# A recurrence's triangular inverse in 16x16 blocks, and its state updated in one pass

## The chip, the cores and the metric

The kernel runs on one core of one Trainium2 chip. The core has a matrix engine (TensorE, PE in the profile), a vector engine (VectorE, DVE), an activation engine (ScalarE, ACT), a general engine (GpSimd, POOL) and SyncE (SP), which here only issues DMAs. Each engine works through its own instructions in order, and semaphores tie the engines together. The metric is the device time of one execution in microseconds, the median of several runs.

## The reference

A two-layer diffusion backbone runs over 512 latent and 256 context tokens of width 1024, batch 1. Each layer normalizes, projects its input to three token mixers and three gates, merges the mixers by the gates, and ends with a SwiGLU block. The third mixer is the one changed, a bidirectional recurrence with 8 heads of 64:

```python
def step(S, inp):                                   # one token
    w_t, k_t, v_t, kk_t, a_t = inp[:5]
    sa = jnp.einsum('bhvk,bhk->bhv', S, kk_t)
    S = S * w_t[:, :, None, :] - sa[..., None] * (kk_t * a_t)[:, :, None, :] + v_t[..., None] * k_t[:, :, None, :]
    return S, jnp.einsum('bhvk,bhk->bhv', S, inp[5])
```

It runs forward and backward, first over the context, then from that state over the latents.

## The kernel before

The kernel doesn't step by tokens. Tokens are taken in chunks of 32, four chunks to a group of 128, so that each direction (`f`, `b`) has six groups and 24 chunks (`SEQ`). Within a chunk the subtraction of `sa` couples the 32 tokens; it becomes a product with the inverse of a triangular 32x32 matrix for each head.

Class `Rwkv` does this with generators that run beside each other:

- `loads` and `prep` fetch a group's decays and keys, scale them, and make `X`: the products of keys within a chunk (`xp` on PE, masked by DVE), 128 rows, with the triangular matrices in its columns 0 to 31. `tp` and `bkt` are the keys transposed. The products go to the PSUM slot `a`, two banks, shared by `xp`, `tp` and the tails.
- `invert` takes a pair of groups, one of each direction, which hold 32 matrices a direction (4 chunks, 8 heads). It sends the matrices through DRAM (`d1`) into `L`, where each stands on 4 partitions; in `G` each of the 4 holds every fourth row of the inverse. `G` starts as the unit matrix, loaded anew. Then come 31 steps on DVE: multiply a column of `G` by a row of `L` into `ftmp`, subtract from `G`. `G` goes through DRAM (`d2`) into `TT`, in the layout that PE wants. Each step needs the one before.
- `chain` is the recurrence, chunk by chunk. PE makes `yp` from the values and from the state `S` (`sblkf`, `sblkb`), ScalarE negates it into `ysb`, PE multiplies by the inverse (`up`), ScalarE copies that to `uv`, PE makes the increment `sp`, and DVE adds it to the state's decayed copy `sc` (L1751). The copy is made as soon as the old state stands, by DVE, GpSimd or ScalarE (L1716, L1719). `op` and `ys` are the outputs.
- `tails` normalize and gate the outputs (`ty`, `gp`).

Beside them, `Kern.beside` runs the big products that fill PE: 16 gate projections (`px` over the 512 latents and, in layer 0 alone, `pz` over the context), then 8 branch projections over the first two mixers' outputs, whose operands `y` are loaded when the gates are done. Each product is three matmuls, of a high and a low part of both factors. A half weight unit is loaded to `raw`, split by ScalarE (`wh`) and by DVE or GpSimd (`wl`); it serves 12 `px`.

Class `Flow` sets the order. Each generator yields an `Op` with its engine, an assumed cost, what it reads and writes, and which slots it takes and gives. Flow takes the operation that could begin first by its own accounting, with a bias for each generator (`F.add(gen, bias, first)`; `first` counts until the first state is written). Engines then follow that order. What follows Flow in a layer is the third branch's projection (`last_branch`), which needs the tails.

Of the kernel before, what the change touches and what calls it, by code (L numbers as in the profile page):

```python
# [28 lines left out]
class Kern:  # L29
# [457 lines left out]
    def beside(self, F, l, n, W):  # L487

        nc, I = self.nc, self.I
        for tag, bufs in (("raw", 3), ("w", 2), ("gx", 2), ("gat", 3)):  # L490
            F.slot(tag, bufs)
# [4 lines left out]
        def raw():  # L496
            for j, src in enumerate(srcs):
                for e in range(2):
                    yield Op("SP", 0.55, (), ("raw", j, e), take=(("raw", (j, e)),), lat=3.5)
                    raws[j, e] = W.tile([128, 512], F32, name="raw", tag="raw", bufs=3)  # L500
                    nc.sync.dma_start(raws[j, e], src[:, 512 * e:512 * e + 512])
# [781 lines left out]
class Rwkv:  # L1283
# [40 lines left out]
    def open(self):  # L1324
        K, nc, l, I = self.K, self.nc, self.l, self.I
        e = self.ctx.enter_context
        self.P = P = e(K.pool(f"rP{l}", side="right"))
        self.T2 = e(K.pool(f"rE{l}", side="right"))
        self.T = self.ctx_t.enter_context(K.pool(f"rT{l}", side="right"))
        self.ps = e(K.pool(f"rps{l}", space=PSUM))  # L1330
        def ld(name, shape, src):
            t = P.tile(shape, F32, name=name)
            nc.sync.dma_start(t, src)
            return t
        self.wg2 = ld("wg2", [128, 512], I["wg2"][l])
        self.gnw = ld("gnw", [128, 128], I["gnw"][l])
        self.gnb = ld("gnb", [128, 128], I["gnb"][l])
        self.masks = ld("rmask", [128, 2, 64], I["rmask"])
        self.smask = P.tile([128, 16, 34], F32, name="smask")
# [174 lines left out]
    def streams(self, F):  # L1514

        self.n = n = {"f": 2 if self.zout else 3, "b": 3}
        for d in "fb":
            for tag, bufs in (("cp", 1), ("kr", n[d]), ("bk", 1), ("pc", 4), ("X", n[d]), ("bkt", 2), ("TT", 2), ("uv", 2), ("ysb", 1), ("ys", 2)):
                F.slot(tag + d, bufs)
        for tag, bufs in (("cs", 1), ("a", 2), ("yu", 2), ("o", 1), ("s", 1), ("d1", 4), ("d2", 4), ("L", 1), ("G", 1), ("tail", 2)):  # L1520
            F.slot(tag, bufs)
# [4 lines left out]
        for d in "fb":  # L1526
            F.add(self.loads(d), 0.15, 1.5)
        for d in "fb":
            F.add(self.chain(d), 0.0)
        for d in "fb":  # L1530
            F.add(self.load_v(d), 0.0)
            F.add(self.prep(d), 0.2, 1.5)
        F.add(self.invert(), 0.2, 1.5)
        F.add(self.tails(), 0.4)
# [29 lines left out]
    def prep(self, d):  # L1564
# [6 lines left out]
        for i, g in enumerate(self.SEQ[d]):  # L1571
# [15 lines left out]
            last = 32 if d == "f" else 1  # L1587
            E = yield Op((("DVE", 0.9), ("POOL", 1.5)), 0, (k("Pe"), k("kr")), k("krn"), take=(("pc" + d, i),))
            kr = h["kr"]
# [28 lines left out]
            for e in range(2):  # L1618
                yield Op("DVE", 0.7, (k("xp%d" % e),), k("X%d" % e), give=(("a", k(e)),), psum=True)
                if not e:  # L1620
                    X = h["X"] = T.tile([128, 2, 2, 4, 64], F32, name="X", tag="X" + d, bufs=self.n[d])
                nc.vector.tensor_tensor(out=X[:, e, :, :, 0:nI].rearrange("q w p i -> q (w p) i"), in0=xp[e][:, :, 0:nI],
# [15 lines left out]
    def invert(self):  # L1638


        nc, T = self.nc, self.T
        for i in range(6):
            k = lambda name, d="": (name, d, i)
            gs = {d: self.SEQ[d][i] for d in "fb"}
            yield Op("ACT", 0.45, (), k("G"), take=(("G", i),), lat=3.3)
            G = T.tile([128, 2, 8, 32], F32, name="G", tag="G", bufs=1)
            nc.scalar.dma_start(G, self.I["gid"])
            d1, L = {}, None
            for z, d in enumerate("fb"):
                g = gs[d]  # L1650
                for q in range(2):
                    yield Op("SP", 0.55, (("X1", d, g),), k("d1%d" % q, d), take=() if q else (("d1", k(0, d)),), lat=3.7)
                    if not q:
                        d1[d] = self.D.tile([2, 16, 32, 32], F32, name="d1", tag="d1", bufs=4)
                    X = self.hs[d, g]["X"]
                    r0 = 0 if q == 0 else 96
                    nc.sync.dma_start(d1[d][q].rearrange("u j i -> j u i"), X[r0:r0 + 32].rearrange("j e w p i -> j (e w p) i")[:, :, 0:32])
                yield Op("SP", 0.55, (k("d10", d), k("d11", d)), k("L", d), take=() if z else (("L", i),), give=(("d1", k(0, d)),), lat=4.2)
                L = L or T.tile([128, 2, 32, 32], F32, name="L", tag="L", bufs=1)
                nc.sync.dma_start(L[:, z].rearrange("u j i -> u (j i)"), d1[d].rearrange("q u j i -> (q u) (j i)").unsqueeze(1).to_broadcast([32, 4, 1024]))  # L1660
            tmp = None
            for n in range(31):
                a, m = n // 4 + 1, 31 - n
                yield Op("DVE", 2 * (0.158 + 0.00105 * 2 * a * m), (k("L", "f"), k("L", "b"), k("G")), k("T"), give=(("L", i),) if n == 30 else ())
                if tmp is None:
                    tmp = T.tile([128, 256], F32, name="ftmp", tag="ftmp", bufs=1)
                t = tmp[:, 0:2 * a * m].rearrange("q (d a b) -> q d a b", d=2, b=m)
                o = G[:, :, 0:a, n + 1:32]
                nc.vector.tensor_tensor(out=t, in0=G[:, :, 0:a, n:n + 1].to_broadcast([128, 2, a, m]), in1=L[:, :, n:n + 1, n + 1:32].to_broadcast([128, 2, a, m]), op=ALU.mult)  # L1669
                nc.vector.tensor_tensor(out=o, in0=o, in1=t, op=ALU.subtract)  # L1670
            for z, d in enumerate("fb"):
                for s in range(4):
                    yield Op("SP", 0.55, (k("T"),), k("d2%d" % s, d), take=() if s else (("d2", k(0, d)),), give=(("G", i),) if s == 3 and z else (), lat=2.5)
                    if not s:
                        d2 = self.D.tile([8, 4, 32, 32], F32, name="d2", tag="d2", bufs=4)
                    nc.sync.dma_start(d2.rearrange("m p (a s) i -> s (m p) a i", s=4)[s], G[s::4, z])
                yield Op("SP", 0.55, tuple(k("d2%d" % s, d) for s in range(4)), ("TT", d, gs[d]), take=(("TT" + d, i),), give=(("d2", k(0, d)),), lat=3.4)
                TT = self.hs[d, gs[d]]["TT"] = T.tile([128, 8, 32], F32, name="TT", tag="TT" + d, bufs=2)
                nc.sync.dma_start(TT, d2.rearrange("m p r i -> (p r) m i"))

    def chain(self, d):
# [3 lines left out]
        for i, g in enumerate(self.SEQ[d]):  # L1685
# [3 lines left out]
            for n in range(4):  # L1689
# [21 lines left out]
                nc.scalar.mul(ysb, yp, -1.0)  # L1711
                if S is not None:
                    E = yield Op((("DVE", 0.75), ("POOL", 1.36), ("ACT", 1.56)), 0, (("S", d),), k("sc"))
                    if E == "ACT":
                        for p in range(4):
                            nc.scalar.activation(self.sc[d][:, p, :], S[:, p, :], AF.Copy, scale=pc[:, p, cl:cl + 1])  # L1716
                    for e in range(0 if E == "ACT" else 2):
                        rr = slice(64 * e, 64 * e + 64)
                        (nc.vector if E == "DVE" else nc.gpsimd).tensor_tensor(out=self.sc[d][rr, :, 64 * e:64 * e + 64], in0=S[rr, :, 64 * e:64 * e + 64],  # L1719
                                                in1=pc[rr, :, cl:cl + 1].to_broadcast([64, 4, 64]), op=ALU.mult)  # L1720
                yield Op("PE", 0.2, (k("ysb"), ("TT", d, g)), k("up"), take=(("yu", k(1)),), give=(("ysb" + d, k(0)),))
# [30 lines left out]
                self.st[d] = Sn  # L1752
# [217 lines left out]
def _consts():  # L1970
# [23 lines left out]
    C["rmask"] = m  # L1994
    g = np.zeros((128, 2, 8, 32), f)
    for s_ in range(4):
        for a in range(8):
            g[s_::4, :, a, 4 * a + s_] = 1
    C["gid"] = g

    T = np.arange(512)
# [117 lines left out]
```

## Time and profile before

| | |
|---|---|
| median of 3 runs | 3251.05 us (3240.05 to 3264.98) |
| profiled execution, its own time | 3247.46 us |
| span of its trace | 3245.6 us |
| mean granted TensorE clock | 0.934 |
| PE busy | 2951.2 us (91%) |
| DVE busy | 1760.7 us (54%) |
| ACT busy | 1202.0 us (37%) |
| POOL busy | 558.7 us (17%) |

A busy share is an average over stages that have different limits. The two stretches in which Flow's order runs lie at about 658 to 1097 us (layer 0) and 2353 to 2756 us (layer 1). The span is from the first to the last instruction, 1.9 us less than the execution's time. [...]

### The profile page before, as it was taken

The numbers are of one execution on the slowest core, as the hardware profiler recorded it, in microseconds if no ns is written. First come the engines' busy times: TensorE is split into PE (matmuls) and PEld (weight loads), VectorE is DVE, ScalarE is ACT, GpSimd is POOL, SyncE is SP. The second block draws the span as 40 slices with busy tenths as digits, with TensorE's granted clock in tenths as the row PEclk, the third lists the DMA queues.
The fourth block names the chain that finished last, engine by engine and source line by source line (L and its number), as shares of the span: only waits on it lengthen the run. The fifth ranks groups of instructions, "written<-read, shape, count | busy, mean of one in ns | idle before, by whom it ended". The sixth has DMA issues, their size and how long they took to land. (4 is left out here: it accounts for less than half of the span.)

```text
span 3245.6 us, 62087 instructions
## 1 busy us (share of the span) xinstructions
PE 2951.2 (91%) x25760; PEld 2362.6 (73%) x25760; DVE 1760.7 (54%) x3455; ACT 1202.0 (37%) x2498; POOL 558.7 (17%) x429
## 2 busy tenths in 40 slices
PE   6999999879989889999999899889779887899998
PEld 3777877657767678888888787667556665888887
DVE  3185666766786745222223536646567767653335
ACT  3154454435443333212112434444335444332223
POOL 3033212200001222101001203212200111220102
PEclk9999999889989989999999899989889885899999
DMA  7421322355455542443222322213365652623333
GB/s 292 159 77 59 105 73 106 106 168 157 144 161 163 163 159 91 147 160 134 62 65 79 106 78 82 76 69 104 134 187 162 183 154 62 201 72 98 93 102 117
DMA packets 276282, 398.30 MB, mean 123 GB/s; under 512 B 96928, under 2 KB 178592, under 8 KB 276000
## 3 DMA queue, kind: packets, MB, share of 16 engines
q1 hardware_dynamic: 250528, 360.77, 34.9%
q10 hardware_dynamic: 25472, 33.56, 3.1%
q8 instruction: 202, 3.31, 0.4%
q14 instruction: 80, 0.66, 0.1%
HBM read 320.33 MB, written 73.92 MB: 121 GB/s over the span
## 5 line engine op out<-in xcount | busy, mean ns | idle before, releaser
L50 PE MATMUL px<-hh,wh 128*128 128x512 f32 x1584 | 644.3, 407 | 14.8 <-ACT gat L473 4.6
L50 PE MATMUL px<-hl,wh 128*128 128x512 f32 x1584 | 636.8, 402 | 9.2 <-POOL hl L302 7.9
L50 PE MATMUL px<-hh,wl 128*128 128x512 f32 x1584 | 636.8, 402 | 5.8 <-DVE wl L510 3.1
L71 ACT ACTIVATE wh<-raw 128x1024 fp32r<-128x1024 f32 (+1 forms) x266 | 275.5, 1039 | 722.4 <-PE pz L50 375.6
L72 DVE TENSOR_TENSOR wl<-raw,wh 128x1024 fp32r<-128x1024 f32 (+1 forms) x266 | 333.0, 1253 | 341.5 <-ACT wh L71 311.5
L50 PEld LDWEIGHTS px<-hh,wh 128*128 128x128 f32 x1584 | 304.3, 192 | 105.3 <-issue 25.8
L50 PEld LDWEIGHTS px<-hh,wl 128*128 128x128 f32 x1584 | 304.1, 192 | 81.6 <-issue 8.0
L50 PEld LDWEIGHTS px<-hl,wh 128*128 128x128 f32 x1584 | 304.1, 192 | 77.3 <-POOL hl L302 13.1
L50 PE MATMUL pz<-hh,wl 128*128 128x256 f32 x872 | 250.7, 288 | 1.3 <-DVE wl L72 0.8
L50 PE MATMUL pz<-hh,wh 128*128 128x256 f32 x872 | 249.9, 288 | 2.1 <-DVE fs L729 1.4
L50 PE MATMUL pz<-hl,wh 128*128 128x256 f32 x872 | 250.0, 287 | 1.9 <-DVE hl L304 1.4
L739 POOL TENSOR_TENSOR al<-fs,ah 128x768 fp32r<-128x768 f32 (+1 forms) x44 | 85.0, 1931 | 727.8 <-ACT ah L738 727.8
L50 PE MATMUL px<-y,wh 128*128 128x512 f32 (+1 forms) x512 | 158.8, 395 | 35.1 <-ACT y L123 13.6
L50 PEld LDWEIGHTS pz<-hh,wh 128*128 128x128 f32 x872 | 167.3, 192 | 10.9 <-issue 2.3
L50 PEld LDWEIGHTS pz<-hl,wh 128*128 128x128 f32 x872 | 168.1, 193 | 9.1 <-issue 2.0
L50 PEld LDWEIGHTS pz<-hh,wl 128*128 128x128 f32 x872 | 168.0, 193 | 6.0 <-issue 3.9
L50 PEld LDWEIGHTS px<-y,wh 128*128 128x128 f32 x512 | 96.1, 211 | 58.7 <-ACT y L123 14.3
L1736 ACT COPY uv<-up 32x128 f32<-32x128 f32 x384 | 98.1, 255 | 69.6 <-PE up L1727 57.6
L50 PE MATMUL px<-ah,wh 128*128 128x512 f32 x296 | 116.1, 393 | 0.0
L1670 DVE TENSOR_TENSOR G<-G,ftmp 128x120 f32<-128x120 f32 (+24 forms) x372 | 108.8, 293 | 12.8
L1669 DVE TENSOR_TENSOR ftmp<-G,L 128x120 f32<-128x120 f32 (+24 forms) x372 | 107.3, 288 | 15.4 <-DMA L<-d 5.3
L50 PE MATMUL px<-ah,wl 128*128 128x512 f32 x296 | 115.3, 390 | 0.0
(460 smaller groups left out, 5776.1 us busy)
## 6 DMA issues: line engine op xcount, KB each, us to landing
raw<-w SPq DMA_DIRECT2D x104, 512.0 KB, 3.5
araw<-wada SPq DMA_DIRECT2D x96, 512.0 KB, 5.0
raw<-win SPq DMA_DIRECT2D x82, 512.0 KB, 3.5
raw<-w SPq DMA_DIRECT2D x48, 448.0 KB, 3.4
raw<-win SPq DMA_DIRECT2D x64, 256.0 KB, 3.4
kr<-krd SPq DMA_DIRECT2D x24, 512.0 KB, 4.9
L<-d SPq DMA_DIRECT2D x24, 512.0 KB, 4.5
gs<-gat ACTq DMA_DIRECT2D x24, 384.0 KB, 3.1
```

Of the source, the lines that this page charges most:

```text
L50: return self.nc.tensor.matmul(out, lhsT=lhsT, rhs=rhs, start=start, stop=stop)
L71: nc.scalar.activation(h[:, :n], raw[:, :n], AF.Copy)
L72: nc.vector.tensor_tensor(out=lo[:, :n], in0=raw[:, :n], in1=h[:, :n].bitcast(F32), op=ALU.subtract)
L739: nc.gpsimd.tensor_tensor(out=al, in0=s, in1=ah.bitcast(F32), op=ALU.subtract)
L1669: nc.vector.tensor_tensor(out=t, in0=G[:, :, 0:a, n:n + 1].to_broadcast([128, 2, a, m]), in1=L[:, :, n:n + 1, n + 1:32].to_broadcast([128, ...
L1670: nc.vector.tensor_tensor(out=o, in0=o, in1=t, op=ALU.subtract)
L1736: nc.scalar.copy(uv[ru, p].rearrange("q e v -> q (e v)"), up[32 * p:32 * p + 32, :])
```

## The change

There are four parts.

1. `invert` works on the two 16x16 blocks on the diagonal of each 32x32 matrix. The 64 blocks of a direction have 2 partitions each, `L` shrinks to a quarter and `G` to a half, and 15 steps replace 31. The blocks go to fixed DRAM tensors that are zeroed at the start of the layer, so that `TT` arrives with both inverses on its diagonal and zeros beside them. Twice as many smaller DMAs write `d1`.
2. A new generator, `finish`, makes the remaining block for each group and direction, as inverse times block times inverse: `ep` transposes `TT` by PE, `qp` multiplies by `X`, `fp` by `TT` once more, with copies by ScalarE between (`E`, `Q`), and a DVE pass adds the result to `TT` with the sign in `other`.
3. In `chain` the decayed copy is gone. DVE updates each of the state's four columns of heads by one pass that multiplies by the decay and adds the increment, on 64 partitions at a time: eight passes for two additions.
4. Numbers: `raw` has two buffers instead of three, `kr` and `X` of the forward direction in layer 0 three instead of two, the lead `first` is 1.0 instead of 1.5, and one GpSimd cost is 1.0 instead of 1.5.

```diff
-        for tag, bufs in (("raw", 3), ("w", 2), ("gx", 2), ("gat", 3)):
+        for tag, bufs in (("raw", 2), ("w", 2), ("gx", 2), ("gat", 3)):
...
-        self.n = n = {"f": 2 if self.zout else 3, "b": 3}
+        self.n = n = {"f": 3, "b": 3}
...
-        F.add(self.invert(), 0.2, 1.5)
+        F.add(self.invert(), 0.2, 1.0)
+        for d in "fb":
+            F.add(self.finish(d), 0.1, 1.0)
...
-            for n in range(31):
-                a, m = n // 4 + 1, 31 - n
-                yield Op("DVE", 2 * (0.158 + 0.00105 * 2 * a * m), (k("L", "f"), k("L", "b"), k("G")), k("T"), give=(("L", i),) if n == 30 else ())
+            for n in range(15):
+                a, m = n // 2 + 1, 15 - n
+                yield Op("DVE", 2 * (0.17 + 0.0012 * 2 * a * m), (k("L", "f"), k("L", "b"), k("G")), k("T"), give=(("L", i),) if n == 14 else ())
...
+    def finish(self, d):
...
+        for i, g in enumerate(self.SEQ[d]):
+            k = lambda name: (name, d, i)
+            yield Op("PE", 0.9, (k("D"),), k("ep"), take=(("a", k("e")), ("E", k(0))))
...
+            for m in range(8):
+                nc.tensor.matmul(ep[rows[m // 4], m % 4, :], lhsT=TT[:, m, :], rhs=K.ident, start=True, stop=True, skip_group_check=True)
+            yield Op("ACT", 1.2, (k("ep"),), k("E"), give=(("a", k("e")),))
...
+            for r in rows:
+                nc.scalar.copy(E[r], ep[r])
+            for q, r in enumerate(rows):
+                yield Op("PE", 0.4, (k("E"),), k("qp%d" % q), take=(("a", k("q%d" % q)),) + (() if q else (("Q", k(0)),)), give=(("E", k(0)),) if q else ())
...
+                for m in range(4):
+                    for p in range(4):
+                        nc.tensor.matmul(qp[32 * p:32 * p + 32, m, :], lhsT=X[r, m // 2, m % 2, p, 0:32], rhs=E[r, m, 32 * p:32 * p + 32], start=True, stop=True, skip_group_check=True)
+                yield Op("ACT", 0.3, (k("qp%d" % q),), k("Q%d" % q), give=(("a", k("q%d" % q)),))
...
+            for m in range(8):
+                for p in range(4):
+                    r = slice(32 * p, 32 * p + 32)
+                    nc.tensor.matmul(fp[r, m, :], lhsT=Q[r, m // 4, m % 4, :], rhs=TT[r, m, 16:32], start=True, stop=True, skip_group_check=True)
+            yield Op("DVE", 0.35, (k("fp"),), ("TT", d, g), give=(("a", k("p")),), psum=True)
+            o = TT[:, :, 16:32]
+            nc.vector.scalar_tensor_tensor(out=o, in0=fp, scalar=self.other[:, 0:1], in1=o, op0=ALU.mult, op1=ALU.add)
...
-                if S is not None:
-                    E = yield Op((("DVE", 0.75), ("POOL", 1.36), ("ACT", 1.56)), 0, (("S", d),), k("sc"))
...
-                yield Op("DVE", 0.88, (k("sp"),) + (() if S is None else (k("sc"),)), ("S", d), give=(("s", k(0)),), psum=True)
+                yield Op("DVE", 0.88 if S is None else 1.6, (k("sp"),), ("S", d), give=(("s", k(0)),), psum=True)
...
-                    else:
-                        nc.vector.tensor_tensor(out=o, in0=sp[rr], in1=self.sc[d][rr, :, 64 * e:64 * e + 64], op=ALU.add)
+                    for p in range(0 if S is None else 4):
+                        nc.vector.scalar_tensor_tensor(out=o[:, p], in0=o[:, p], scalar=pc[rr, p, cl:cl + 1], in1=sp[rr, p], op0=ALU.mult, op1=ALU.add)
```

Flow makes a new order of it, and three places of that follow. The first is PE in layer 0, where the recurrence's first `up` stands. Before, it had only gate products (`px`, `pz`) around it:

```order
L50 MATMUL pz<-hl_144,wh 128x256
L50 MATMUL pz<-hh_136,wl 128x256
L50 MATMUL pz<-hh_137,wh 128x256
L50 MATMUL pz<-hl_145,wh 128x256
L1727 MATMUL up<-ysb,TT 32x64 x8
L50 MATMUL pz<-hh_137,wl 128x256
```

After, at the same place:

```order
L50 MATMUL px<-hh_138,wh 128x512
L1704 MATMUL ep<-ident,TT 32x128 x8
L1724 MATMUL fp<-TT,Q 32x16 x32
L50 MATMUL px<-hl_146,wh 128x512
L50 MATMUL px<-hh_138,wl 128x512
L50 MATMUL pz<-hh_135,wh 128x256
L1766 MATMUL up<-ysb,TT 32x64 x8
L1714 MATMUL qp<-E,X 32x32 x16
L50 MATMUL pz<-hl_143,wh 128x256
```

The end of the forward direction's finish (`fp`) now stands three products ahead of the first `up`, and the backward direction's finish (`ep`, `qp`) runs among them. The second place is DVE at the first updates of the state, a little later. Before, the scaled copies (`scf`, `scb`) stand between the updates:

```order
L1579 SCALAR_TENSOR_TENSOR cs<-smask,cp 128x544
L1749 COPY sblkf<-sp 64x4x64 x2
L1719 TENSOR_TENSOR scf<-sblkf,pc 64x4x64 x2
L1591 COPY pc<-cp 128x16
L1594 TENSOR_TENSOR kr<-kr,cp 128x16x32
L510 TENSOR_TENSOR wl<-raw,wh 128x512
L1597 TENSOR_TENSOR kr<-kr,cp 128x16x32
L1751 TENSOR_TENSOR sblkf<-sp,scf 64x4x64 x2
L1749 COPY sblkb<-sp 64x4x64 x2
L1719 TENSOR_TENSOR scb<-sblkb,pc 64x4x64 x2
```

After:

```order
L1788 COPY sblkf<-sp 64x4x64 x2
L1589 SCALAR_TENSOR_TENSOR cs<-smask,cp 128x544
L510 TENSOR_TENSOR wl<-raw,wh 128x512
L1727 SCALAR_TENSOR_TENSOR TT<-fp,rother,TT 128x8x16
L1607 TENSOR_TENSOR kr<-kr,cp 128x16x32
L1790 SCALAR_TENSOR_TENSOR sblkf<-sblkf,pc,sp 64x64 x8
L1616 TENSOR_TENSOR bk<-bk,cs 128x8x64
L1616 TENSOR_TENSOR bk<-bk,cs 128x8x2x32
L1788 COPY sblkb<-sp 64x4x64 x2
L1632 TENSOR_TENSOR X<-xp,rmask 128x512
L1681 TENSOR_TENSOR ftmp<-G,L 128x30
L1682 TENSOR_TENSOR G<-G,ftmp 128x2x15
```

The copies are gone, an update is eight instructions, a finish's last step (`TT<-fp`) stands between, and the next pair's inverse begins sooner. The third place is PE in layer 1, in the last but one group. Before, all products stand ahead of it:

```order
L1727 MATMUL up<-ysb,TT 32x64 x8
L1759 MATMUL op<-uv,X 32x64 x8
L1703 MATMUL yp<-uv,X 32x64 x8
L1733 MATMUL op<-sblkb,kr 32x128 x4
L1708 MATMUL yp<-sblkf,kr 32x128 x4
L50 MATMUL sp<-uv,bkt 64x64 x8
```

After:

```order
L1766 MATMUL up<-ysb,TT 32x64 x8
L1772 MATMUL op<-sblkb,kr 32x128 x4
L50 MATMUL px<-y_1_3_1_27580,wh 128x512
L50 MATMUL px<-y_1_3_0_27579,wl 128x512
L50 MATMUL px<-y_0_0_0_26701,wh 128x512
L50 MATMUL px<-y_0_0_1_26702,wh 128x512
L50 MATMUL px<-y_0_0_0_26701,wl 128x512
L50 MATMUL px<-y_0_1_0_26821,wh 128x512
L50 MATMUL sp<-uv,bkt 64x64 x8
L50 MATMUL px<-y_0_1_1_26822,wh 128x512
L1798 MATMUL op<-uv,X 32x64 x8
```

Branch products now stand between the recurrence's pieces in this group. Counted through the order: before, 16 `up` follow the last product of layer 1, after, 8. In layer 0 the last `up` stood behind all products of Flow; after, 156 `px` and 159 `pz` follow it, and seven `up` in a row stand between the last gate product and the first branch product, where before there was one. The products ahead of the first `up` are 72 `px` and 61 `pz` in layer 0, before and after; in layer 1 there are 33 `px` more.

## Rows read from the trace of the kernel before

**Rows 1.** Windows: each engine's busy time (instructions), then clock, DMA share, GB/s.

```profile
658.10:717.60 59.50, 45.96 (x460) 38.75 (x460) 42.15 (x96) 15.27 (x28) 3.85 (x3) 0.78 0.55 164
717.60:950.00 232.40, 226.38 (x3680) 173.42 (x3684) 168.07 (x422) 117.67 (x352) 21.64 (x18) 0.97 0.52 154
950.00:1000.00 50.00, 38.00 (x480) 27.11 (x472) 30.27 (x65) 18.05 (x44) 3.14 (x3) 0.75 0.60 175
1097.20:1165.00 67.80, 44.86 (x236) 37.78 (x226) 45.41 (x67) 21.41 (x33) 19.83 (x15) 0.80 0.62 190
2353.50:2410.10 56.60, 38.23 (x455) 30.84 (x455) 43.49 (x100) 15.42 (x27) 3.87 (x3) 0.76 0.60 181
2410.10:2657.20 247.10, 231.17 (x3193) 165.30 (x3193) 182.71 (x437) 125.33 (x357) 31.96 (x25) 0.94 0.58 171
2657.20:2756.10 98.90, 71.53 (x1278) 50.48 (x1277) 62.56 (x176) 35.02 (x125) 8.53 (x7) 0.53 0.29 75
```

**Rows 2.** Waits of PE, 1097.2 to 1165: us in total, times, longest.

```profile
PE px L50 <- ACT y L123: 6.4, 1, 6.4
PE ty L1839 <- DVE ys L1828: 6.3, 1, 6.3
```

**Rows 3.** Waits of PE, 2657.2 to 2756.1.

```profile
PE ty L1839 <- DVE ys L1828: 15.3, 2, 15.0
PE up L1727 <- DMA TT<-d: 9.0, 3, 6.7
```

**Rows 4.** Group of `up` in the whole run: busy us, mean ns; idle before it.

```profile
L1727 PE MATMUL up<-ysb,TT 32*32 32x64 f32 x1536 | 46.1, 241 | 20.3 <-DMA TT<-d 16.2 <-ACT ysb L1711 4.1
```

**Rows 5.** Timeline of PE, products of layer 0: start us, duration us.

```profile
1044.37 0.39 PE L50 MATMUL px<-y,wl 128*128 128x512 f32 x1
1044.60 0.40 PE L50 MATMUL pz<-y,wh 128*128 128x256 f32 x2
1044.83 0.28 PE L50 MATMUL pz<-y,wl 128*128 128x256 f32 x1
```

**Rows 6.** Timeline of PE, small matmuls of the recurrence at full clock.

```profile
1054.25 0.43 PE L1727 MATMUL up<-ysb,TT 32*32 32x64 f32 x16
1054.60 0.43 PE L1733 MATMUL op<-sblkf,kr 128*32 128x128 f32 x8
1054.96 0.39 PE L50 MATMUL pz<-y,wh 128*128 128x256 f32 x1
...
1056.48 0.68 PE L50 MATMUL sp<-uv,bkt 64*64 64x64 f32 x16
1057.09 1.16 PE L50 MATMUL gp<-tsgl,wg 128*128 128x128 f32 x8
```

**Rows 7.** Timeline of PE, small matmuls of the first mixer.

```profile
344.88 1.02 PE L50 MATMUL gsc<-gD,gD 64*32 64x32 f32 x96
```

**Rows 8.** Timelines of DVE and ACT: updates of a state, and scaling ahead of `uv`.

```profile
326.12 1.47 DVE L962 SCALAR_TENSOR_TENSOR gSf<-gSf,gtot,gsp 64x128 f32<-64x128 f32 x4
...
944.85 0.86 DVE L1751 TENSOR_TENSOR sblkb<-sp,scb 64x256 f32<-64x256 f32 x2
...
946.42 1.26 ACT L1716 ACTIVATE scb<-sblkb,pc 128x128 f32<-128x128 f32 x4
947.59 1.08 ACT L1736 COPY uv<-up 32x128 f32<-32x128 f32 x4
```

**Rows 9.** Inverse on DVE: first and last instruction in layer 1; a group by shape.

```profile
2376.94 0.23 DVE L1669 TENSOR_TENSOR ftmp<-G,L 128x62 f32<-128x62 f32 x1 [0.65 <-DMA L<-d]
...
2401.72 0.19 DVE L1670 TENSOR_TENSOR G<-G,ftmp 128x16 f32<-128x16 f32 x1
...
L1669 DVE TENSOR_TENSOR ftmp<-G,L 128x56 f32<-128x56 f32 x24 | 5.2, 216 | 0.6
```

**Rows 10.** Timeline of DVE, updates of the forward state in layer 1's tail.

```profile
2666.68 0.88 DVE L1751 TENSOR_TENSOR sblkf<-sp,scf 64x256 f32<-64x256 f32 x2 [7.42 <-PE sp L50]
...
2687.79 0.86 DVE L1751 TENSOR_TENSOR sblkf<-sp,scf 64x256 f32<-64x256 f32 x2
```

**Rows 11.** DMA issues: count, KB each, median us to landing.

```profile
raw<-win SPq DMA_DIRECT2D x64, 256.0 KB, 3.4
```

More of the change, by code (lines that the diff above doesn't have):

```diff
@@ L1338, in open @@
         self.masks = ld("rmask", [128, 2, 64], I["rmask"])
+        self.other = self.T.tile([128, 1], F32, name="rother")
+        nc.sync.dma_start(self.other, I["other"])
+        zero = self.T.tile([128, 256], F32, name="zero")
+        nc.gpsimd.memset(zero, 0.0)
+        self.d2 = {d: [self.D.tile([8, 4, 32, 32], F32, name=f"d2{d}{i}") for i in range(2)] for d in "fb"}
+        for d in "fb":
+            for t in self.d2[d]:
+                nc.sync.dma_start(t.rearrange("m p (x r) i -> (m p x) (r i)", x=4), zero)
         self.smask = P.tile([128, 16, 34], F32, name="smask")
@@ L1587, in prep @@
             last = 32 if d == "f" else 1
-            E = yield Op((("DVE", 0.9), ("POOL", 1.5)), 0, (k("Pe"), k("kr")), k("krn"), take=(("pc" + d, i),))
+            E = yield Op((("DVE", 0.9), ("POOL", 1.0)), 0, (k("Pe"), k("kr")), k("krn"), take=(("pc" + d, i),))
             kr = h["kr"]
@@ L1658, in invert @@
-                yield Op("SP", 0.55, (k("d10", d), k("d11", d)), k("L", d), take=() if z else (("L", i),), give=(("d1", k(0, d)),), lat=4.2)
-                L = L or T.tile([128, 2, 32, 32], F32, name="L", tag="L", bufs=1)
-                nc.sync.dma_start(L[:, z].rearrange("u j i -> u (j i)"), d1[d].rearrange("q u j i -> (q u) (j i)").unsqueeze(1).to_broadcast([32, 4, 1024]))
+                    for h in range(2):
+                        yield Op("SP", 0.55, (("X1", d, g),), k("d1%d" % (2 * q + h), d), take=() if q or h else (("d1", k(0, d)),), lat=3.0)
+                        if not q and not h:
+                            d1[d] = self.D.tile([2, 2, 16, 16, 16], F32, name="d1", tag="d1", bufs=4)
+                        X = self.hs[d, g]["X"]
+                        r0 = (0, 96)[q] + 16 * h
+                        nc.sync.dma_start(d1[d][h, q].rearrange("u j i -> j u i"), X[r0:r0 + 16].rearrange("j e w p i -> j (e w p) i")[:, :, 16 * h:16 * h + 16])
@@ L1670, in invert @@
+                nc.vector.tensor_tensor(out=t, in0=G[:, :, 0:a, n:n + 1].to_broadcast([128, 2, a, m]), in1=L[:, :, n:n + 1, n + 1:16].to_broadcast([128, 2, a, m]), op=ALU.mult)
                 nc.vector.tensor_tensor(out=o, in0=o, in1=t, op=ALU.subtract)
             for z, d in enumerate("fb"):
[L1672 to L1676, printed above, removed]
@@ L1677, in invert @@
-                yield Op("SP", 0.55, tuple(k("d2%d" % s, d) for s in range(4)), ("TT", d, gs[d]), take=(("TT" + d, i),), give=(("d2", k(0, d)),), lat=3.4)
+                d2 = self.d2[d][i % 2]
+                to = d2.rearrange("m p (h a s) i -> h s (m p) a i", h=2, s=2)
+                for h in range(2):
+                    for s in range(2):
+                        yield Op("SP", 0.55, (k("T"),), k("d2%d" % (2 * h + s), d), give=(("G", i),) if h + s + z == 3 else (), lat=2.5)
+                        nc.sync.dma_start(to[h, s][:, :, 16 * h:16 * h + 16], G[64 * h + s:64 * h + 64:2, z])
@@ L1994, in _consts @@
     C["rmask"] = m
-    g = np.zeros((128, 2, 8, 32), f)
-    for s_ in range(4):
+    g = np.zeros((128, 2, 8, 16), f)
+    for s_ in range(2):
         for a in range(8):
-            g[s_::4, :, a, 4 * a + s_] = 1
+            g[s_::2, :, a, 2 * a + s_] = 1
     C["gid"] = g
+    C["other"] = np.where(p % 32 < 16, -1.0, 0.0)[:, None].astype(f)
     T = np.arange(512)
```

48 lines of the change are left out of this document (25 added, 23 removed).

## The prediction

> **What bounds the kernel now.** I read the profile in this order: first the windows of the two stretches in which the third mixer's recurrence runs, then what TensorE (PE) waited for in them, then single rows for durations. Nothing outside these stretches changes but set-up loads, so the sum is made over them alone.
>
> In the windows the reader should compare PE with VectorE (DVE). In layer 0, from the first `up` at 717.6 to 950, PE is busy 226.4 of 232.4 us at a clock of 0.97, and DVE 168.1 [rows 1]. PE is the bound there: what is added to its work is added to the time, and a lighter DVE gives nothing. The picture changes three times. Before the first `up` (59.5 and 56.6 us) DVE has 42.2 and 43.5 us of work and PE stands at clocks of 0.78 and 0.76. From 950 to 1000, where the gate products have run out and the projections' operands are not there yet, PE has 38.0 us at 0.75. And in layer 1, from 2657.2 on, no product is left: the recurrence runs alone for 98.9 us at a clock of 0.53, though the inverse is late for it [rows 1]. There PE waits 15.3 us for a tail's DVE work and 9.0 us for `TT` from its DMA [rows 3]. Behind the recurrence of layer 0, PE waits another 6.4 and 6.3 us for operands and a tail [rows 2].
>
> So two limits take turns: PE's work in the mixed stretches, and the path inverse, `TT`, recurrence where products are missing. The change adds to the first and rearranges the second.
>
> **The change part by part.**
>
> *The finish on PE.* One finish writes 8 + 32 + 32 = 72 small fp32 matmuls; the trace shows two instructions for each (eight `up` are x16 there). An `up` of 16 takes 0.35 us up to the next instruction, eight instructions of 128x128 on 32 columns 0.36 [rows 6]; 96 of 64x32 take about 1 us, near 10 ns each [rows 7]. Each switch between products and small tiles costs some 0.13 us in these distances (16 at 14 ns is 0.22). So `ep`, 16 at 22 ns, is 0.48; `qp`, twice 32 at 12 ns, 1.02; `fp`, 64 at 12 ns, 0.90: 2.4 us. 24 finishes are **+58 us**, of which 29 in layer 0. The ends: 2.15 us each with `qp` and `fp` at the pace of the 64x32 row (52 in all), 3.7 with 22 ns for all (88). All of it counts, since the finishes stand among products where PE has no idle time; in the tail of layer 1 the last two stand on the recurrence's path.
>
> Row 7's 10 ns is the price of a small matmul here. [...]
>
> *The tail of layer 1.* Before, 16 `up` follow the last product, in 98.9 us. In the new order eight do; the other eight stand between products. Alone and undisturbed, one direction took three steps between its updates at 2666.68 and 2687.79, 7.0 us each [rows 10]; four steps and half a step for the other direction are 32 us. The eight steps that move among products cost PE 2.4 us each (two `yp`, `up`, two `op`, `sp`: 0.36 x 4 + 0.35 + 0.6 [rows 6]), 19 us. 98.9 - 32 - 19 is 48 us at most, nothing at least, if the inverse still paces the steps ahead. I take **-40**, near the upper end, because the 15.3 us wait for a tail lies in this stretch and the new order puts that tail's `ty` elsewhere.
>
> *The end of layer 0.* 156 px and 159 pz products now stand behind the last `up`; at 0.23 and 0.115 us each [rows 5] they are 54 us, enough to cover the two waits of [rows 2]: **-13** (nothing at the other end). They were due anyway.
>
> *The step from gate products to projections, layer 0.* In the new order seven `up` stand where before there was one and PE idled 12.0 us of 950 to 1000. Those steps are work that is taken out of later stretches: **-12** (0 to -20, with the lower clock).
>
> *The shorter inverse.* 62 DVE instructions become 30, of at most 72 elements; one of 56 takes 0.22 us [rows 9]. The first inverse of layer 1 lasted from 2376.94 to 2401.91 [rows 9], 25 us with what stands between; by the number of instructions 12 remain, so 13 go. The finish puts some 5 back (four PE pieces, three copies and a DVE step with a handover each). Before the first `up` stand as many products as before in layer 0 (72 px, 61 pz), but 33 px more in layer 1, 7.6 us. So **-8** in layer 0, nothing in layer 1 (ends 0 and -16). In the middle, PE waited 16.2 us for `TT` in all [rows 4], 9.0 of it in the tail above: **-7** (0 to -7).
>
> *The state in one pass.* Two additions of 64x256 took 0.86 us together; four passes of the same kind as the new one, on 64x128, took 1.47, 0.37 apart [rows 8]. The new ones have 64 elements: between the 0.22 of 56 elements and 0.37; I take 0.30, eight are 2.4, so each update is 1.5 us longer. Where the scaling ran on ScalarE it stood 1.26 us ahead of `uv` [rows 8], which is now free; I count 0.4 a step. Each update stands between `sp` and the next `yp` of its direction. Among products PE has 2 to 3 us of other work there, which hides it. It is bare where no product stands: 7 in layer 0, 8 + 7 in layer 1, 22 `up` or 11 steps of a direction: 11 x 1.1 = **+12**. The ends: 0, and +69 if all 46 updates of a direction wait.
>
> [...]
>
> DVE in all: 736 passes for 184 additions and 66 scalings is about +110 us, 360 inverse steps for 744 about -130. It is as full as before, only otherwise; I cost that at nothing.
>
> *Two `raw` buffers instead of three.* A half unit lands in 3.4 us [rows 11] and is then split in two. Before, in most of the stretch, PE's own pace held the buffers. In runs of products without steps (104, 107 and 66 px in layer 1, 12 px or 2.8 us for each half) the third one was used: **+4** (0 to 14). The four more d1 issues a pair on SyncE's queue and the smaller DMAs I cost at nothing; that queue idles here.
>
> **How the sum stands.** 58 - 40 - 13 - 12 - 8 - 7 + 12 + 4 = **-6 us**. The profiled execution took 3247.5 us (a span of 3245.6), 3.6 under the median of 3251.05; so 3241 profiled and about **3245** for the median.
>
> **Rivals.**
> - *The state's update is late everywhere.* If an update ends after PE has come to `yp`, PE stands, with all products behind it in its queue. The new order leaves 2 to 3 us between, against 2.4 plus handovers; from 0.35 us a pass on it decides. For: [rows 8]'s spacing. Against: only 64 elements. All 46 bare instead of 11: +57, **3302**.
> - *The inverse paced more than I allow.* For: DVE is busy 183 of 247 us in the mixed stretch of layer 1 [rows 1], and the steps of the inverse stand one by one among that. If PE's idle time there (16 us, and the clock of 0.94) and at the changes of work goes as the inverse gets 13 - 5 = 8 us shorter in five of six groups, -40: **3205**. Against: PE is near full in layer 0.
> [...]
>
> **How the numbers follow.** The forecast has 0.50, with a range of its own from 3213 to 3277 by the ends of its terms taken half together; the late update 0.21, the pacing inverse 0.23, the floor 0.06. Reaching to the first two rivals, the range is 3180 to 3305. Of no change a measurement can tell about 1%, 32 us. Faster by over 1%: 0.09 of the forecast and 0.20 of the inverse's case, 0.29; slower: 0.04, 0.19 and 0.03, 0.26; within 1%: 0.45.
>
> **What would show it.** In the new profile a finish should take 2.1 to 3.7 us of PE; the state's eight passes 1.8 to 2.9; the stretch after layer 1's last product 30 to 45 us; in 1097 to 1165's successor no wait for `ty` over 2 us; PE's waits for the state near 12 us in sum. I am wrong if those waits reach 40 us, if PE waits for the finish's copies (nothing is counted for them), or if the mixed stretch of layer 0 does not grow by PE's 20 to 30 us.

## The result, and the profile after

| | before | after |
|---|---|---|
| median | 3248.7 us (14 runs) | 3282.9 us (14 runs) |
| ratio, with its 95% interval | | 1.0096 (1.0079 to 1.0113) |
| span of the profiled execution | 3245.6 us | 3285.3 us |

The kernel became 31 to 34 us slower, where 6 us less was forecast. It lies inside the stated range, but on the other side of no change.

Three pairs of rows hold the account. The first are the windows of the two stretches, from the first product of keys (`xp`) to the same product of the merge behind the recurrence (length, busy time of PE, PEld, DVE, ACT and POOL, then the granted TensorE clock as a share of full speed, DMA share and GB/s). Of the kernel before:

```profile
658.10:1220.50 562.40, 502.83 (x6384) 394.01 (x6384) 384.02 (x869) 225.06 (x597) 75.69 (x59) 0.92 0.52 158
2353.60:2842.10 488.50, 412.23 (x5440) 315.00 (x5441) 343.75 (x810) 208.04 (x563) 67.79 (x61) 0.82 0.53 157
```

Of the changed kernel:

```profile
666.30:1245.60 579.30, 547.82 (x8112) 427.71 (x8112) 345.25 (x933) 212.28 (x533) 66.53 (x55) 0.93 0.48 142
2387.70:2882.20 494.50, 455.19 (x7168) 342.40 (x7169) 299.72 (x861) 196.57 (x499) 80.16 (x71) 0.86 0.48 141
```

PE is busy 45 and 43 us longer, 88 together, and idle 28 and 37 us less (562.4 - 502.8 against 579.3 - 547.8, and so on), 65 together: the stretches grew by 16.9 and 6.0 us. Another 14 lie ahead of them: measured from the same product of the set-up, the first `xp` came 6.0 us later in layer 0 and 8.2 in layer 1. PE waited there for its first operands. In layer 0, before and after (waits of PE: us in total, times, longest):

```profile
PE xp L50 <- issue: 7.9, 1, 7.9
...
PE xp L50 <- DVE bk L1612: 13.8, 1, 13.8
```

In layer 1 the same wait went from 7.3 to 14.4 us, so 13 of the 14 are these two waits.

SyncE's queue of the changed kernel in layer 0 shows where the operands were held:

```profile
633.33 0.80 SPq L1346 DMA_DIRECT2D d2f<-zero  x2
645.20 11.53 SPq L1346 DMA_DIRECT2D d2b<-zero  x2
656.77 0.56 SPq L1556 DMA_DIRECT2D cp<-twdf  x1
657.37 0.65 SPq L1559 DMA_DIRECT2D kr<-krd  x1
658.12 0.57 SPq L1562 DMA_DIRECT2D bk<-bkdf  x1
```

Before, `cp` went out at 631.46 and `bk` at 642.39. The zero fills now stand ahead, and the last of them left only at 656.4, as an unrelated `uv<-vtok` landed.

The second pair is the finish and the state. In the whole run (busy us, mean ns, then idle before):

```profile
L1704 PE MATMUL ep<-ident,TT 128*32 128x128 f32 x384 | 41.4, 297 | 11.4 <-DMA TT<-d2f 8.5 <-issue 2.5 <-ACT tsq L1874 0.3
...
L1714 PE MATMUL qp<-E,X 32*32 32x32 f32 x1536 | 23.1, 199 | 1.3 <-ACT E L1708 0.9 <-ACT bkt L1646 0.3
L1724 PE MATMUL fp<-TT,Q 32*32 32x16 f32 x1536 | 19.4, 186 | 1.2 <-issue 1.2
```

From start to start of the next instruction the 24 finishes are 81.0 us (42.0, 20.3 and 18.6); 5 of these are idle time behind them. One `ep` with what follows it, and one update, from the timelines of PE and DVE:

```profile
822.79 1.53 PE L1704 MATMUL ep<-ident,TT 128*32 128x128 f32 x16
824.25 0.42 PE L1751 MATMUL yp<-uv,X 32*32 32x64 f32 x16
...
732.45 1.76 DVE L1790 SCALAR_TENSOR_TENSOR sblkf<-sblkf,pc,sp 64x64 f32<-64x64 f32 x8 [4.16 <-PE sp L50]
```

`ep` takes 1.46 us, three times the 0.48 forecast. The eight passes take 1.76, not 2.4, which is 0.22 a pass on average (0.20 apart within a half, 0.28 where the half changes). That lies at the lower end of the 0.22 to 0.37 between which I took 0.30.

The third are the three stretches in which few products or none stand: from the last gate product to the 37th branch product of each layer, and from the last branch product within the recurrence of layer 1 to the next one. Before:

```profile
942.30:984.10 41.80, 27.92 (x344) 19.82 (x343) 29.75 (x72) 17.89 (x43) 1.24 (x2) 0.67 0.61 180
2539.80:2589.50 49.70, 43.03 (x703) 30.57 (x702) 35.85 (x96) 25.45 (x80) 4.07 (x3) 0.73 0.62 187
2657.20:2757.90 100.70, 71.53 (x1278) 50.48 (x1277) 64.30 (x179) 36.51 (x127) 8.53 (x7) 0.53 0.29 76
```

After:

```profile
988.40:1052.40 64.00, 59.49 (x1424) 41.62 (x1422) 42.88 (x156) 33.35 (x103) 1.27 (x1) 0.84 0.40 115
2591.90:2673.80 81.90, 77.00 (x1427) 54.43 (x1423) 45.20 (x152) 33.37 (x99) 10.36 (x8) 0.67 0.39 114
2743.90:2797.50 53.60, 45.62 (x955) 34.07 (x950) 36.52 (x131) 20.69 (x64) 5.66 (x5) 0.65 0.25 76
```

The tail shrank by 47 us, where 40 was forecast, to 53.6 (the prediction's sign was 30 to 45). The other two grew by 22 and 32. The waits of [rows 2, 3] for `ty` and `TT` are gone from these places; behind layer 0's recurrence PE's longest wait is 4.5 us, for a `gl`. None of the prediction's three conditions for being wrong came true: PE's waits for the state are 3.9 us, those for the finish's copies 0.9, and layer 0's mixed stretch did grow (first `up` to last gate product, 224.7 to 267.9 us). They did not look at the places that went wrong.

### The profile page after: what moved, and what is told of

Its sections match the earlier page's. It is cut to its first block, busy times and chain, and to the rows that moved or that the text cites. A ratio compares the mean times of both kernels' runs of the same rounds, so it can differ in the third digit from the quotient of the medians.

```text
span 3285.3 us, 69122 instructions
## 1 busy us (share of the span) xinstructions
PE 3041.5 (93%) x29216; PEld 2426.2 (74%) x29216; DVE 1676.0 (51%) x3569; ACT 1177.8 (36%) x2370; POOL 562.1 (17%) x437
## 5 line engine op out<-in xcount | busy, mean ns | idle before, releaser
L50 PE MATMUL px<-y,wh 128*128 128x512 f32 (+1 forms) x512 | 156.3, 391 | 28.2 <-ACT y L123 10.1
L510 POOL TENSOR_TENSOR wl<-raw,wh 128x512 fp32r<-128x512 f32 x35 | 45.1, 1289 | 510.8 <-ACT wh L508 438.7
L1790 DVE SCALAR_TENSOR_TENSOR sblkb<-sblkb,pc,sp 64x64 f32<-64x64 f32 x368 | 80.4, 280 | 91.9 <-PE sp L50 90.7
L1790 DVE SCALAR_TENSOR_TENSOR sblkf<-sblkf,pc,sp 64x64 f32<-64x64 f32 x368 | 80.4, 280 | 79.5 <-PE sp L50 78.5
```

The source lines that it names most:

```text
L50: return self.nc.tensor.matmul(out, lhsT=lhsT, rhs=rhs, start=start, stop=stop)
L510: (nc.vector if E == "DVE" else nc.gpsimd).tensor_tensor(out=lo, in0=r, in1=h.bitcast(F32), op=ALU.subtract)
L1790: nc.vector.scalar_tensor_tensor(out=o[:, p], in0=o[:, p], scalar=pc[rr, p, cl:cl + 1], in1=sp[rr, p], op0=ALU.mult, op1=ALU.add)
```

## Experiments

Times are medians; ratios are to the kernel before, run beside on the same chip. Single runs of one kernel lie up to 37 us apart, so that a difference below some 10 us is not told apart here by medians. The runs are called e1 to e18, in the order in which they were put on record.

**The zero fills later (e1).**

```diff
-        for d in "fb":
-            for t in self.d2[d]:
-                nc.sync.dma_start(t.rearrange(...), zero)
...
+            if i == 0:      # in invert, behind the loads of L
+                for d in "fb": ...
```

> The changed kernel, with the eight zero fills of the DRAM tensors issued behind the first pair's loads of L instead of ahead of all loads of the recurrence; nothing else differs, nothing is left out. Theory 1 (in the changed kernel the fills hold SyncE's queue: the second fill of d2b went out at 656.4 us, and the first products of keys began 6 us later after the second mixer's last product than before in layer 0, 8 us later in layer 1, and nothing gives that back): 12 to 14 us less than the changed kernel, about 3270, PE's gap ahead of the first xp back to 8 us in layer 0. Rival (the first inverse or the gate products absorb the delay): the gap closes, the time stays within 4 us of the changed kernel's 3283.

3274.8 us, 1.0076 (1.0052 to 1.0101). In layer 0 PE's wait ahead of the first `xp` is 8.0 us again; in the trace 6 and 7 us of the two set-ups are gone. The median shows 8 of the 13, which by itself is within the noise.

**`ep` over two column groups (e2).** A column group here is a set of 32 partitions that a matmul writes; the eight of `ep` write two such sets, in the changed kernel first four times the one, then four times the other.

```diff
-            for m in range(8):
+            for m in (0, 4, 1, 5, 2, 6, 3, 7):
                 nc.tensor.matmul(ep[rows[m // 4], m % 4, :], ...
```

> The changed kernel, with the eight matmuls of ep issued in the order 0, 4, 1, 5, 2, 6, 3, 7, so that neighbours write different quarters of the PSUM rows; the order on every engine is otherwise the same, nothing is left out. In the changed kernel ep takes 1.53 us of PE in layer 0 and 1.97 in layer 1, 42 us for 24, where 0.48 each was forecast from the rate of up. Theory 1 (neighbours of ep share a column group and run one after another, 95 ns an instruction, where op of 128x128 on 32 columns goes at 45 because its neighbours lie in different groups): ep falls to 0.75 to 0.95 us, 18 to 25 us less in all, about 3262. Rival 1 (the price is that of the columns streamed, whatever the group): ep and the time stay. Rival 2 (the finish is not on PE's path): ep falls, the time stays within 5 us of 3283.

3270.3 us, 1.0064 (1.0036 to 1.0092). The timeline:

```profile
779.94 1.07 PE L1704 MATMUL ep<-ident,TT 128*32 128x128 f32 x16
780.94 0.50 PE L50 MATMUL px<-hh,wh 128*128 128x512 f32 x1
```

1.00 us instead of 1.46; over the run `ep` fell from 42.0 to 29.4 and the median by 12.6. So the group matters, though by less than theory 1's half. The median fell by as much as PE's time; the two ratios' intervals still overlap, so that this alone is not clear of the noise.

**The state's two operations instead of the one pass (e3)** (the lines of `sc` and the addition as before, the cost 0.88).

> The changed kernel with the state's update of before (decayed copy on DVE, GpSimd or ScalarE, and one addition a half), that is the new inverse, its finish and the numbers alone; nothing is left out. The measured state pass is 0.28 us each, eight 2.2 us, where the two additions took 0.86. Theory 1 (the late update is bare only where no product stands, the term of +12 us): 5 to 15 us less than the changed kernel, about 3273. Rival 1 (the one-pass update is late everywhere): 30 us less or more, about 3250. Rival 2 (the one pass frees DVE and ScalarE and gains): 5 to 20 us more, 3288 to 3303.

3261.2 us, 1.0030 (1.0008 to 1.0052): 22 us less, between theory 1 and rival 1. The planner also made another order of it.

**The one pass alone, in the kernel before (e4).**

> The kernel before with only the state's one-pass update; the inverse of 32x32 and the numbers are those of before, nothing is left out. Theory 1: +5 to +15 us on 3249, about 3260. Rival 1 (late everywhere): +40 to +60, about 3300. Rival 2 (it frees DVE, which in this kernel carries the long inverse): 5 to 20 us less, 3229 to 3244.

3286.7 us, 1.0118 (1.0085 to 1.0151): 35 more, between theory 1 and rival 1. Here too the order is another (products come earlier, the end of layer 1 is longer), so price and order are mixed. The next runs part them.

**The one pass in the order of the two operations (e5; e13 and e14 are two more pairs in one order).**

```diff
+                    E = yield Op((("DVE", 0.75), ("POOL", 1.36), ("ACT", 1.56)), 0, (("S", d),), k("sc"))   # nothing is made
-                yield Op("DVE", 0.88 if S is None else 1.6, (k("sp"),), ...
+                yield Op("DVE", 0.88, (k("sp"),) + (() if S is None else (k("sc"),)), ...
```

> The order of the kernel with the two-op state (the run before of that name, 3261 us) with the state's update in one pass: the planner still counts 0.88 us for the update and a decayed copy, which is not made; in the two stretches the big products and the recurrence's pieces stand in the same row on PE. Nothing is left out. This parts the price of the passes from the order that the planner makes of its new cost of 1.6 us. Theory 1 (price: eight passes of 0.28 us stand between sp and the next yp, and PE waits for them): 3275 to 3290, like the changed kernel. Theory 2 (order: the new cost of 1.6 puts the recurrence later behind the products): within 6 us of 3261.

3275.4 us, 1.0097 (1.0077 to 1.0116): 14 us more than e3 by medians, 22 by ratios. That is theory 1: the price is there without a new order. PE's lines of the `yp` that read the state, e3 and then e5:

```profile
L1756 PE MATMUL yp<-sblkf,kr 128*32 128x128 f32 x368 | 22.4, 308 | 0.9 <-issue 0.9
...
L1756 PE MATMUL yp<-sblkb,kr 128*32 128x128 f32 x368 | 21.3, 307 | 0.5 <-DVE sblkb L1797 0.4
...
L1756 PE MATMUL yp<-sblkb,kr 128*32 128x128 f32 x368 | 28.1, 304 | 3.4 <-DVE sblkb L1792 2.6 <-DVE sblkb L1790 0.4
L1756 PE MATMUL yp<-sblkf,kr 128*32 128x128 f32 x368 | 26.6, 302 | 3.0 <-DVE sblkf L1792 2.1 <-issue 0.8
```

> The order of the kernel with the inverse alone (3276 us; two-op state, numbers of before) with the state's update in one pass and no decayed copy; the order of the products and of the recurrence on PE is the same, nothing is left out. Theory 1 (in a given order the one pass costs 14 to 22 us, as it did in the other order): 3288 to 3300. Theory 2 (its price goes with the order; planned for itself under these numbers the one pass came out at 3270): 3266 to 3282.

3287.0 us, 1.0104 (1.0072 to 1.0136): e13 is 11 more than e9 (the inverse alone, below), 8 by ratios: just short of theory 1.

> The changed kernel's order with the state's two operations: the decayed copy goes out on DVE right behind the negation of yp, not planned, and the addition stands where the one pass stood; nothing is left out. The reverse of the last but one test. Theory 1: 14 to 22 us less than the changed kernel, 3260 to 3270. Theory 2 (the changed kernel's order, made for the one pass, gains nothing from the shorter update): 3278 to 3290.

3275.7 us, 1.0072 (1.0044 to 1.0100): e14 is 7 less than the changed kernel, between the two theories. In the three pairs PE's time at the `yp` that reads the state, from start to start, grew by 10.1, 9.3 and 6.7 us (41.2 to 51.3, 39.5 to 48.8, 39.5 to 46.2). With PE's idle time ahead of them it grew by 15.0, 14.0 and 7.3, much as the times did (14, 11 and 7). Only the first pair's intervals lie apart; all go one way.

**The update cut in sixteen (e10)** (`sblk` in pieces of 32 columns, in e5's order).

> The run with the one pass in the old order (3275 us), with each update cut into sixteen passes of 64x32 instead of eight of 64x64; the order of the big products and of the recurrence on PE is the same, nothing is left out. Eight passes took 2.2 us, sixteen should take 3.8 to 4.0. Theory 1 (the time between sp and the next yp is paid, at the rate at which 1.4 us more for each of 92 updates gave some 15 to 22 us): 18 to 30 us more, 3293 to 3305. Rival (what the one pass costs is something else than its length, as the scaling that stood on other engines): within 8 us of 3275.

3349.3 us, 1.0302 (1.0263 to 1.0341): 74 more than e5, beyond both theories. The update, and the `yp` behind it (lines of DVE and PE):

```profile
731.12 2.81 DVE L1793 SCALAR_TENSOR_TENSOR sblkf<-sblkf,pc,sp 64x32 f32<-64x32 f32 x16 [4.15 <-PE sp L50]
...
L1756 PE MATMUL yp<-sblkb,kr 128*32 128x128 f32 x368 | 49.6, 303 | 12.0 <-DVE sblkb L1793 11.6 <-DVE sblkb L1790 0.4
```

From 0.86 to 1.76 us an update added 0.90 x 92 = 83 us and 7 to 14 were paid; from 1.76 to 2.81 it added 97 and 74 were paid. Of these, 54 stand at the `yp` that read the state, with the idle time ahead of them; where the other 20 lie is open. The cover of 2 to 3 us that the prediction counted for updates among products is there, and ends near 2 (an estimate: 2.81 less 74 / 92).

**The numbers of before (e6), then the buffers of before alone (e11).**

> The changed kernel with the numbers of before: three buffers of raw, two of kr and X for the forward direction in layer 0, a lead of 1.5, and 1.5 for the cost on GpSimd; nothing is left out. Theory 1 (the numbers matter little; two buffers of raw were forecast at 4 us): 3275 to 3287. Rival 1 (products wait for raw, which the third buffer takes away): 10 us or more less, under 3272. Rival 2 (the lead of 1.0 is what keeps the recurrence early): over 3293.

> The changed kernel with the buffers of before alone (raw three, kr and X of the forward direction in layer 0 two); the lead of 1.0 and GpSimd's cost of 1.0 stay; nothing is left out. Theory 1 (of the 10 us that the old numbers gave, the third raw buffer is the larger part): 3272 to 3278. Rival (the lead gave it): 3280 to 3287.

e6: 3269.5 us, 1.0072 (1.0046 to 1.0099); e11: 3277.8, 1.0085 (1.0056 to 1.0113). By their intervals neither is told apart from the changed kernel. With the old buffers the 384 `px` of gates in layer 0 took 103.7 us in e11 and 105.4 in e6, instead of 115.0 (from start to start; 105.8 in the kernel before), so two buffers seem to hold products; e11's stretch in layer 1 came out 10 us longer in its order.

**The inverse alone (e9)**, with the state's operations and the numbers of before.

> The kernel before with the first two parts of the change alone: the inverse of 16x16 blocks and its finish, with the state's two operations and the numbers of before; nothing is left out. By the runs so far the one pass costs 22 us and the numbers some 8, so theory 1: 3243 to 3253, no measurable change, since the 81 us of the finish on PE buy back about as much waiting. Rival 1 (the prediction's own terms for the inverse, +58 - 40 - 13 - 12 - 8 - 7): 3227. Rival 2 (the late zero fills and the slow ep come out in full): 3262 or more.

3275.6 us, 1.0080 (1.0052 to 1.0107). Rival 2: +26 us by the ratio, where the prediction's own terms made -22.

**Mends.** First the two-op state, late fills and alternating `ep` (e7); then also `ep` of half the columns (e8):

```diff
-                nc.tensor.matmul(ep[rows[m // 4], m % 4, :], lhsT=TT[:, m, :], rhs=K.ident, ...
+                nc.tensor.matmul(ep[rows[m // 4], m % 4, :], lhsT=TT[:, m, :], rhs=K.ident.rearrange("q (p s) -> q p s", s=32)[:, :, 0:16], ...
```

> The changed kernel with the two-op state, the late zero fills and the alternating ep together, which is before with the new inverse, its finish, the numbers and two mends; nothing is left out. Theory 1 (the three are apart from each other: -22, -8 and -13 us): 3240, 0.997 of before. Rival (they mend the same wait): about 3255.

> The run with three mends, and a finish of half the columns: only the rows of the inverse that the finish adds to are transposed, so that ep streams 64 columns instead of 128, qp 16 instead of 32, and the copies are half as wide; the result is the same. Theory 1 (PE's time in the finish goes into the time one to one, ep by its columns): ep 0.5 to 0.6 us each instead of 1.1, 10 to 14 us less than the run with three mends, about 3228. Rival (ep is bound by its weights or its count): under 4 us less.

e7: 3246.1 us, 0.9989 (0.9970 to 1.0008), between theory and rival. e8: **3234.5 us, 0.9973 (0.9959 to 0.9987)**, its theory 1, and faster than both kernels. `ep` now:

```profile
773.33 0.64 PE L1708 MATMUL ep<-ident,TT 128*32 128x64 f32 x16
773.90 0.73 PE L1728 MATMUL fp<-TT,Q 32*32 32x16 f32 x64
```

Over the run it fell from 27.3 to 14.5 us; `qp`, with 16 columns instead of 32, stayed (23.9 and 24.2 from start to start; 19.0 and 18.5 without the idle time behind).

The same with the numbers of before (e12):

> The run with three mends and the finish of half the columns (3234 us), with the numbers of before. Theory 1 (the numbers give here what they gave the changed kernel): 3222 to 3230, 0.994 of before. Rival (with the shorter update the lead and the third raw buffer no longer matter): 3231 to 3238.

3257.6 us, 1.0026 (1.0008 to 1.0045), 23 slower than with the new numbers; neither theory held.

The mends with the one pass (e15):

> The changed kernel, one pass and new numbers, with the zero fills late, the alternating ep and the finish of half the columns; the order is that of the changed kernel, nothing is left out. If the finish's price and the first loads are two terms of their own (-8, -13 and -12 us in other runs), theory 1: 3247 to 3257, and what is left against the same mends with the two-op state (3234 us) is the one pass, 13 to 23 us. Rival (the one pass is the limit, and shorter work on PE only turns into longer waits for the state): 3262 or more.

3264.4 us, 1.0055 (1.0032 to 1.0079): the rival's side. The finish is 59.2 us of PE instead of 81.0, and the 14 us of late loads are gone: 36 us, of which the median shows 18. In its two stretches PE is busy 35 us less than in the changed kernel and idle 16 more. (The trace is of its fastest execution, 3249 us.)

**The branch products' operands in a row (e16 in the changed kernel, e17 in e8, e18 in the kernel before).** In the changed kernel the eight `y` were split over 38 and 59 us, in between the recurrence's steps.

```diff
+        def ys():          # the loop over yraw, out of after()
...
+        F.add(ys(), -3.0)
```

> The changed kernel, with the eight loads and splits of the branch products' operands y taken out of the generator that also stores the gates and given a generator of their own with a lead of 3, so that the planner sets them in a row behind the last gate product; nothing is left out. In the changed kernel they lie 38 us apart in layer 0 and 59 in layer 1, among the recurrence's steps, where before they took 18 and 28; from the last gate product to the 37th branch product go 64.0 and 81.9 us, where before it was 41.8 and 49.7, at clocks of 0.84 and 0.67. Theory 1 (this spread is where the shorter tail of layer 1 was given back: bare steps on PE at a low clock while products wait for operands): both stretches 15 to 25 us shorter, the time 10 to 25 us less, 3258 to 3273. Rival (the steps that leave the stretch come out bare at the end of the layer, where the order now has 25 steps behind the first branch product of layer 1 instead of 21): within 7 us of 3283.

3288.2 us, 1.0144 (1.0095 to 1.0192). The same three stretches:

```profile
989.90:1022.40 32.50, 29.55 (x544) 20.69 (x543) 22.19 (x73) 18.87 (x52) 2.54 (x2) 0.89 0.62 180
2583.10:2619.90 36.80, 32.05 (x585) 21.83 (x582) 21.47 (x54) 19.66 (x50) 4.10 (x4) 0.91 0.72 213
2696.00:2793.20 97.20, 81.25 (x1775) 60.33 (x1773) 61.86 (x232) 34.83 (x115) 6.96 (x6) 0.59 0.28 78
```

The first two are 32 and 45 us shorter, and the time is not: the tail is 97 us again, and in layer 0 the last `up` stands 64 us behind the 37th branch product instead of 16. My theory falls. Late operands are not what these steps cost; they have to stand somewhere.

> The fastest kernel so far (three mends, a finish of half the columns, two-op state, 3234 us) with the operands y in a row in the same way; nothing is left out. There they lie 26 and 38 us apart. Theory 1: 5 to 15 us less, 3219 to 3229. Rival: within 5 us of 3234.

> The kernel before with the operands y in a row in the same way; nothing is left out. Both theories: here they lie 18 and 28 us apart already, so within 8 us of 3249; if it gains as much as the changed kernel does, the spread is not what the change brought about.

e17: 3242.2 us, 0.9987 (0.9969 to 1.0005), 8 more than e8 and outside both of its theories; e18: 3250.8, 1.0005 (0.9980 to 1.0031). No gain in either.

## Why the prediction was wrong

From before to after there is a chain of runs: the inverse alone 1.0080 (e9), then the one pass in the same order 1.0104 (e13), then the new numbers with the planner's own order 1.0096. So +26 us, +8 to 11, and about -3; only the first step is clear of the noise. It is one path of several, and the parts do not add. With the numbers of before and each kernel in its own order, the inverse makes +26 us with two operations (e9), but -15 with the one pass (e6 against e4, by ratios). The order that the planner makes thus weighs about as much as any part. By terms:

- *The finish on PE*, +58: **81**. The rate was read from the wrong row. I gave `ep` the 22 ns of `up`, which streams 64 columns and spreads over four groups of columns. The nearer row was in the same group: the 128x128 `op` on 32 columns, 45 ns [rows 6], and `ep` has half its spread and came to 91 to 95. `qp` and `fp` were taken a little dear (most at 0.76 and 0.65 us, where 1.02 and 0.90 were taken). The bounds 52 to 88 held it. The floor for small matmuls, to which I gave 0.06, is shown by no run: those 0.76 and 0.65 us are 12 and 10 ns an instruction, not above the 12 that I counted. The switch between products and small tiles, which I put at 0.13 us, is 0.10 to 0.12 in the trace of before: a `px` took 0.33 us up to an `up` and 0.23 up to the next `px` (2598.20, 2597.97), eight `op` 0.36 up to a product and 0.24 up to a `yp` of the same shape (1054.60, 2609.95).
- *"Nothing outside these stretches changes but set-up loads"*: this failed. The set-up loads stand on the queue that starts the recurrence, SyncE's, of which I wrote that it idles; the first `xp` came 6 and 8 us later (e1: 8 of them in the median). The fills are four issues a layer, and I put them at nothing.
- *The tail of layer 1*, -40, and *the step from gate products to projections*, -12: 47 us left the tail, and 54 came back in the two transitions. Up to the 37th branch product PE had 2 and 7 `up` before and 13 and 11 after; in the tail 16 and 8. Together that is 25 and 32. I booked the eight that left the tail as a gain and the ones in layer 0's transition as a second gain; those in layer 1's I counted in the state's term alone. e16 shows it from the other side: in layer 1 the tail took back 44 us as the transition gave 45.
- *The end of layer 0*, -13, *the shorter inverse*, -8, *TT*, -7: the first two waits are gone; from the first `xp` to the first `up` went 54.2 us instead of 59.5, in layer 1 54.4 instead of 56.6. PE's waits for `TT` fell from 16.2 to 8.5 us, now ahead of `ep`.
- *The state*, +12: 7 to 14 in one order (8 to 22 by ratios). That the size fits is luck in part. With the measured 1.76 us instead of 2.4 the same working gives 11 x (0.90 - 0.4) = 5.5, and there are more bare steps than I counted (32 `up` in the three stretches, not 22). Planned for itself, the one pass came out 35 us dearer in the kernel before (e4), 22 in the changed one (against e3), 27 with the mends (e15 against e8), and 6 cheaper with the numbers of before (e6 against e9). Late in most places, the first rival, is what sixteen passes come near to.
- *Two buffers*, +4: of either sign, as far as the numbers together show. The numbers of before made -13 in the changed kernel (not clear of its noise) and +23 in the fastest.

The terms besides the finish summed to -64, and PE's idle time in the two stretches fell by 65. That agreement is luck in part: e15, with a finish of 59 us and no late loads, is the kernel that the sum describes, and it ran 15 to 18 us above the kernel before, not 6 below. So the finish and the loads are a third to a half of the miss. e8 is e15 with two operations for the state, in an order of its own: 9 to 12 us below the kernel before, where the sum without the state's term has 18 below. Thus the larger part of the rest, some 15 us, goes with the one pass and the order that the planner makes of it (27 us, not 12), and 6 to 9 with the terms on the tail, the transitions and the waits. No run parts price from order there, so for this half the cause stays open.

## What to carry to other kernels

A step that is moved out of a bare stretch is a gain only if the places where it arrives are counted too: count the bare steps of the whole stretch, not those of its tail (here 47 us left the tail and 54 came back). Price a small matmul from a row with its columns and its spread over the array: with neighbours on one group of columns `ep` took 91 ns an instruction, alternating between two groups 63. And a set-up DMA can cost what stands behind it on its queue, small as it is: here fills of 128 KB put the first `xp` of the layers 6 and 8 us back.

## What was not expected

- A fill of 128 KB with nothing to wait for stood 11 us in SyncE's queue and left at 656.4 us, as a DMA of ScalarE's queue landed (`uv<-vtok`, issued at 653.71, 2.7 us to landing). With the fills later (e1), `bk` and `cp` of the same queue stood in that way (issued at 645.40 and 656.54, with waits ahead). What ties the two queues is not shown; no run tests it.
- Other numbers, and with them another order of nearly the same instructions, moved the time as much as parts of the change: those of before were 13 us better with the one pass (e6; within the noise) and 14 to 23 worse with two operations (e9 against e3, e12 against e8).
- Fewer columns did not make `qp` faster (24.2 us over the run at 16, e8; 23.9 at 32, e7). One half of it, 32 instructions, took 0.37 us up to the next instruction at 16 columns (e8, from 776.05) and 0.38 at 32 (e2, from 786.72). What bounds it instead is not shown.
